# The S5 recurrence on VectorE, its output ahead of fewer gate columns, and mLSTM scores in four tiles

## The chip, the cores and the metric

The kernel runs on one core of a Trainium2 chip. The metric is the device time of one execution in microseconds (us). A core has TensorE (PE), VectorE (DVE), ScalarE (ACT), GpSimd (POOL) and SyncE (SP), each with its own in-order instruction stream; in the profile PEld is the loading of weights into TensorE. DMA transfers are issued from the queues of SP, ACT and POOL.

## The reference

One layer of a hybrid block with D = 2048, 256 latent tokens and 256 context tokens. One projection `w_in` of the modulated inputs feeds three branches: a Hyena long convolution, an mLSTM and an S5 state-space model, each 768 wide. Every branch is projected to 2048 and multiplied by its own sigmoid gate (6144 more columns of `w_in`); the sum goes through `w_out`, and a squared-ReLU MLP follows.

```python
hy_c, qk_c, v_c, o_c, gt_c, u_c, mg_c = jnp.split(h_ctx @ w_in, SPLIT_POINTS, axis=-1)
hy_l, qk_l, v_l, o_l, gt_l, u_l, mg_l = jnp.split(h_lat @ w_in, SPLIT_POINTS, axis=-1)
hm_l, _, _ = mlstm_bidir(mlstm_prep(qk_l, v_l, gt_l, ...), mst_f, mst_b)
ys_l, _, _ = s5_bidir(u_l, disc, c_re, c_im, sst_f, sst_b, True)   # x_t = A x_(t-1) + B u_t, both directions
y = y.reshape(B, L, W_S5) + d * u                                  # s5_out
z = jax.nn.gelu(y); y_s5 = z * jax.nn.sigmoid(z @ glu_w + glu_b)
merged = g_hy * (y_hy @ w_hy_out) + g_ml * (y_ml @ w_ml_out) + g_s5 * (y_s5 @ w_s5_out)
x = layer_norm(ALPHA * x + mod[2] * (merged @ w_out)); x = layer_norm(ALPHA * x + mod[5] * mlp(modulate(x)))
```

## The kernel before

**Weights.** Every large product streams its weight matrix from HBM in chunks of 128x1024 (512 KB) on SP's queue into `wr` (four buffers). ACT rounds a chunk to `wh` (L190) and DVE forms the rest `wl = wr - wh` (L194); each has three buffers. TensorE then does 24 matmuls on a latent chunk (hi x hi, hi x lo, lo x hi; L211). The next chunk's `wh` and `wl` can be written once the matmuls on the buffer's last holder are done.

**Order.** The program runs through the modulation `w_mod`, then the columns of `w_in` for K, V, Q, U and O (U feeds S5), the hyena columns `hy` (36 chunks: blocks hy0 to hy3 of eight chunks and hy4 of four), and the 96 chunks of gate columns, here G0 to G11, eight chunks each, whose results go to DRAM (`mg_consume`, stores L1210 on POOL's queue) until the merges read them back. A merge of a branch multiplies its output by its projection and by its gates. After that come `w_out` and the MLP.

**Sides.** `run_steps(steps, n)` writes n chunks of a matrix into the program; after each chunk every registered side generator is advanced by its rate (`with_side(gen, rate)`), and `drain()` writes out what is left of one. A second side, `mod_late`, runs all along: it accumulates the rest of `w_mod` on DVE (`mac`, L1180, two of 128x512 a chunk of its weights). The program's order isn't the engines' order: a list scheduler (`schedule_with_timeline_sim`) fixes each engine's static order from its own simulation, with the program's order as priority.

**S5.** `u_consume` stores U reordered to DRAM (`UD`) and keeps the latent part in the tile `uT`. `s5_inject` forms the input of the states in `S`; `s5_scan` (L644) is a recurrence of 63 dependent steps, four elementwise instructions of 128x96 each (L651 to L654), on POOL. `s5_output` (L659) works through six column tiles: DMA loads of `u`, `KD` and `Q`, eight small copies of the states into one buffer `xb` (four on ACT, four on DVE, L679), 32 matmuls with `Q` (L686), 16 with `tp` (L692), four ACT copies `ye`, 16 matmuls `aux<-consts` (L211), and one DVE instruction that adds d times `uT` (L701, into `z`). After the sixth tile one Gelu on ACT covers all of `z`. `s5_glu` splits `z` into hi and lo (`s5wq<-z`) and multiplies it by the GLU matrix in six chunks, glu0 and glu1 with three each.

**Placing.** In the program before, `s5_scan` is a side (rate 2) under the last 36 hyena chunks, then 32 gate chunks (G0 to G3) follow, `s5_output` is a side at rate 0.6 under 48 more (G4 to G9), then `s5_glu`, the hyena convolution (`hyena`: short DFT products with elementwise work on DVE and POOL between), the last 16 gate chunks (G10, G11) and the merges. `mlstm` writes its scores into `st_all`, one large tile that shares its buffer with tiles used until the U columns are done.

Of the kernel before, what the change touches and what calls it, by code (L numbers as in the profile page):

```python
# [10 lines left out]
F32 = mybir.dt.float32  # L11
# [6 lines left out]
P = 128  # L18
D = 2048
KT = D // P  # L20
T = 256
W = 768
CT = W // P
DFF = 8192
NIN = 12304
HEADS = 4
DH = 192
LC = 8
# [87 lines left out]
class Kern:  # L116
# [482 lines left out]
    def u_consume(self, ct0, nct, ps):  # L599

        for c in range(nct):
            ct = ct0 + c
            up = self.b2([P, LC, 2, 32])
            self.act(up[:, ::-1], ps[:, 2 * c:2 * c + 2, :].rearrange("p s (j i) -> p i s j", i=LC))
            for g in range(8):
                self.nc.scalar.dma_start(self.UD[ct, :, :, g, :].rearrange("i c n -> c i n"),
                                         up[16 * g:16 * g + 16].rearrange("c i s j -> c i (s j)"))
            self.nc.vector.tensor_copy(self.uT[:, ct, :], ps[:, 2 * c + 1, :])

# [34 lines left out]
    def s5_scan(self):  # L644

        v = self.nc.gpsimd
        S = self.S
# [9 lines left out]
    def s5_output(self):  # L657

        nc = self.nc  # L659
        v = nc.vector  # L660
# [5 lines left out]
        for ct in range(CT):  # L666
            u = self.s5_u(ct, self.b2([P, 8, NCH]))
            tp = self.t(self.br, [P, 8, P], "s5tp", 2)
            nc.scalar.dma_start(tp.rearrange("p g n -> p (g n)"), self.KD[:, :, ct].rearrange("i c g n -> (i c) (g n)"))
            Q = self.t(self.br, [P, 2, 2, 4, P], "s5wq", 2)  # L670
            nc.scalar.dma_start(Q.rearrange("p d s q n -> p d (s q n)"),
                                self.QD[ct].rearrange("d p s q n -> p d (s q n)"))
# [26 lines left out]
            for i in range(LC):  # L699
                self.mm(pc[:, i, :], ye[:, i].rearrange("r p g c -> r (p g c)"), self.c("four"), i == 0, True)  # L700
            v.scalar_tensor_tensor(z[:, ct, :].rearrange("p (j i) -> p i j", i=LC),  # L701
                                   self.uT[:, ct, :].rearrange("p (j i) -> p i j", i=LC),
                                   self.s5d[:, ct:ct + 1], pc, op0=ALU.mult, op1=ALU.add)
# [187 lines left out]
    def mlstm(self):  # L891
        nc = self.nc
        v = nc.vector
        st = []
        st_all = self.t32(F32, (P, 4, HEADS, T))
        for sb in range(4):
            s_sb = st_all[:, sb]
            for hp in range(2):
                ps = self.aux([P, 2, T])
# [506 lines left out]
    def run(self):  # L1406
# [4 lines left out]
        self.MG = self.t(self.dr, [12, P, 4, T], "MG")  # L1411
        self.A8 = self.t(self.dr, [P, 192], "A8")
        self.WA = self.t(self.dr, [CT, P, 4, 4, P], "WA")
        self.QD = self.t(self.dr, [CT, 2, P, 2, 4, P], "QD")
# [48 lines left out]
        with self.scope("yp") as self.yp:  # L1463
# [12 lines left out]
            with self.scope("pA") as self.br:  # L1476
# [26 lines left out]
                self.mlstm()  # L1503
                self.uT = self.ty()
                self.lin_w_all(w_in, O_U, W, KT, both, self.u_consume)
# [9 lines left out]
            with self.scope("pB") as self.br:  # L1515
# [6 lines left out]
                self.run_steps(hy, 36)  # L1522
                self.run_steps(steps, 32)
                self.with_side(self.s5_output(), 0.6)
                self.run_steps(steps, 48)
                self.drain()
# [46 lines left out]
```

## Time and profile before

| | us |
|---|---|
| median of 3 runs (lowest, highest) | 2005.19 (2005.02, 2005.46) |
| the profiled execution | 2014.18 |
| its span | 2012.4 |
| PE busy in the span | 1870.4 (93%) |
| DVE busy | 1300.5 (65%) |
| ACT busy | 803.2 (40%) |
| POOL busy | 361.7 (18%) |

Busy times are of the profiled execution. A row of a timeline gives the start from the beginning of the span, the duration of the group, the engine, the line and what is written from what; PEclk is the granted TensorE clock as a share of full speed. Some stretches of PE's row that count as busy run at half the clock, so busy time and work done are not the same there.

### The profile page before, as it was taken

The numbers are of one execution on the slowest core, as the hardware profiler recorded it, in microseconds if no ns is written. First come the engines' busy times: TensorE is split into PE (matmuls) and PEld (weight loads), VectorE is DVE, ScalarE is ACT, GpSimd is POOL, SyncE is SP. The second block draws the span as 40 slices with busy tenths as digits, with TensorE's granted clock in tenths as the row PEclk, the third lists the DMA queues.
The fourth block names the chain that finished last, engine by engine and source line by source line (L and its number), as shares of the span: only waits on it lengthen the run. The fifth ranks groups of instructions, "written<-read, shape, count | busy, mean of one in ns | idle before, by whom it ended". The sixth has DMA issues, their size and how long they took to land.

```text
span 2012.4 us, 34496 instructions
## 1 busy us (share of the span) xinstructions
PE 1870.4 (93%) x13945; PEld 1707.4 (85%) x13945; DVE 1300.5 (65%) x1810; ACT 803.2 (40%) x1063; POOL 361.7 (18%) x534
## 2 busy tenths in 40 slices
PE   5888999999997995999889998999999999999996
PEld 1666988989997995999779877999988899998985
DVE  8985777647866553556786866766755555555556
ACT  2433324226543333544234533444433344444332
POOL 1221101000019994000452400400000000000001
PEclk7898999999998997999999998999999999999998
DMA  9997667775797765677657866577765566666553
GB/s 346 339 344 262 192 202 220 227 208 174 232 349 230 239 222 210 226 254 259 244 180 253 276 225 227 158 240 224 254 224 187 187 183 186 181 186 231 190 188 105
DMA packets 253472, 455.92 MB, mean 227 GB/s; under 512 B 28597, under 2 KB 75349, under 8 KB 251776
## 3 DMA queue, kind: packets, MB, share of 16 engines
q1 hardware_dynamic: 221824, 382.43, 59.4%
q0 software_dynamic: 14112, 50.83, 7.0%
q10 hardware_dynamic: 17376, 20.45, 3.1%
q8 instruction: 109, 1.79, 0.4%
q14 instruction: 51, 0.42, 0.1%
HBM read 424.75 MB, written 32.05 MB: 227 GB/s over the span
## 4 chain that ended last, share of the span: by engine, by line
PE 67%; DMA 10%; DVE 9%; POOL 8%; issue 3%; ACT 2%; SPq 0%; ACTq 0%; POOLq 0%; DVEq 0%
PE mm L211 59%; PE aux L211 4%; DMA wr<-in_w_mod_dram 4%; DVE wl L194 3%; DMA wr<-in_w_in_dram 2%; POOL sc L651 2%; POOL sc L653 2%; POOL sc L652 2%; POOL t L654 2%; DMA wr<-in_w_out_dram 1%; ACT wh L190 1%; PE px L406 1%; PE px L211 1%; PE aux L214 1%; DVE mac L1180 1%
## 5 line engine op out<-in xcount | busy, mean ns | idle before, releaser
L211 PE MATMUL mm<-t,wh 128*128 128x256 f32 x5888 | 1101.7, 288 | 29.0 <-ACT wh L190 18.1
L211 PEld LDWEIGHTS mm<-t,wh 128*128 128x128 f32 x5888 | 932.2, 194 | 49.6 <-ACT wh L190 19.9
L194 DVE TENSOR_TENSOR wl<-wr,wh 128x1024 fp32r<-128x1024 f32 (+1 forms) x517 | 649.6, 1263 | 385.9 <-ACT wh L190 385.4
L190 ACT ACTIVATE wh<-wr 128x1024 fp32r<-128x1024 f32 (+1 forms) x517 | 545.9, 1058 | 811.0 <-PE mm L211 580.6
L211 PE MATMUL mm<-t,wl 128*128 128x256 f32 x2944 | 847.6, 288 | 13.9 <-DVE wl L194 13.8
L211 PEld LDWEIGHTS mm<-t,wl 128*128 128x128 f32 x2944 | 570.1, 194 | 25.9 <-DVE wl L194 18.3
L1180 DVE SCALAR_TENSOR_TENSOR mac<-wr,vecs,mac 128x512 f32<-128x512 f32 x240 | 185.3, 772 | 156.5 <-DMA wr<-in_w_mod_dram 153.8
L211 PE MATMUL mm<-wh,t 128*128 128x512 f32 (+1 forms) x960 | 249.1, 349 | 0.2
L211 PEld LDWEIGHTS mm<-wh,t 128*128 128x128 f32 x960 | 169.0, 190 | 24.2 <-ACT wh L190 1.6
L211 PE MATMUL mm<-wl,t 128*128 128x512 f32 (+1 forms) x480 | 168.0, 350 | 5.5 <-DVE wl L194 5.5
L211 PE MATMUL mm<-wh,ff 128*128 128x512 f32 (+1 forms) x576 | 155.3, 358 | 0.0
L211 PEld LDWEIGHTS mm<-wh,ff 128*128 128x128 f32 x576 | 101.7, 188 | 17.6
L211 PEld LDWEIGHTS mm<-wl,t 128*128 128x128 f32 x480 | 91.3, 190 | 20.5 <-DVE wl L194 9.2
L211 PE MATMUL mm<-wl,ff 128*128 128x512 f32 (+1 forms) x288 | 103.0, 357 | 0.0
L211 PE MATMUL mm<-ty,wh 128*128 128x256 f32 x384 | 73.3, 289 | 0.0
L1402 POOL DMA_DIRECT2D t<-in_ln_g_dram x1 | 0.5, 535 | 355.0 <-PE mm L211 355.0
L211 PE MATMUL mm<-ty,wl 128*128 128x256 f32 x192 | 56.4, 294 | 7.6 <-DVE wl L194 7.5
L211 PEld LDWEIGHTS mm<-wl,ff 128*128 128x128 f32 x288 | 54.2, 188 | 8.8
L211 PEld LDWEIGHTS mm<-ty,wh 128*128 128x128 f32 x384 | 60.7, 192 | 0.9
L406 PE MATMUL px<-wr,b 128*32 128x512 f32 x128 | 41.4, 739 | 18.1 <-DVE s5t L335 10.5
L211 PE MATMUL aux<-t,t 128*128 128x384 f32 (+3 forms) x160 | 47.3, 411 | 7.7 <-DVE t L1146 3.2
L211 PEld LDWEIGHTS mm<-ty,wl 128*128 128x128 f32 x192 | 36.9, 192 | 9.1 <-DVE wl L194 8.4
(384 smaller groups left out, 1621.6 us busy)
## 6 DMA issues: line engine op xcount, KB each, us to landing
wr<-in_w_ff_dram SPq DMA_DIRECT2D x256, 512.0 KB, 3.9
wr<-in_w_in_dram SPq DMA_DIRECT2D x192, 512.0 KB, 4.7
wr<-in_w_mod_dram SPq DMA_DIRECT2D x160, 512.0 KB, 4.8
wr<-in_w_out_dram SPq DMA_DIRECT2D x32, 512.0 KB, 4.7
wh<-in_w_mod_dram SPq DMA_DIRECT2D x16, 512.0 KB, 7.6
wl<-in_w_mod_dram SPq DMA_DIRECT2D x16, 512.0 KB, 7.1
QD<-s5Q POOLq DMA_DIRECT2D x12, 512.0 KB, 7.1
WA<-s5wa POOLq DMA_DIRECT2D x24, 256.0 KB, 6.2
```

The source lines that it names most:

```text
L190: return self.nc.scalar.activation(out, in_, f, bias=bias, scale=scale)
L194: self.nc.vector.tensor_sub(lo, x, hi.bitcast(F32))
L211: self.nc.tensor.matmul(out, lhsT, rhs, start=start, stop=stop, skip_group_check=True)
L214: self.nc.tensor.transpose(out, in_, self.c("ident", n)[:, :n])
L406: nc.tensor.matmul(ps[o:o + 32], self.st[:, k, :], raw[:, kk, :], start=k < 4, stop=k >= KT - 4, skip_group_check=True, tile_position=(0, o))
L651: v.tensor_mul(t1, self.a8[:, 0], S[:, :, :, :, n - 1])
L652: v.tensor_mul(t2, self.a8[:, 1], S[:, :, ::-1, :, n - 1])
L653: v.tensor_add(t1, t1, S[:, :, :, :, n])
L654: v.tensor_add(S[:, :, :, :, n], t1, t2)
L1180: v.scalar_tensor_tensor(acc, x, c, acc, op0=ALU.mult, op1=ALU.add)
L1402: nc.gpsimd.dma_start(g2r, I["ln2_g"].to_broadcast([P, D]))
```

## The change

Four edits. The recurrence `s5_scan` is issued on DVE instead of POOL. The latent part of U is no longer kept in `uT`: `u_consume` copies it into a short-lived tile and stores it to the DRAM tensor `UL` by POOL's queue (six stores), and `s5_output` loads it back by ACT's queue (six loads). The mLSTM's scores go into four tiles of the pool `ty` in place of the one large tile. And the placing: 16 gate chunks (G0, G1) follow the hyena columns, then `s5_output` is a side at rate 0.4 under 16 more (G2, G3), is drained, and `s5_glu` and the hyena convolution follow; the remaining 64 gate chunks (G4 to G11) come behind them in the program.

```diff
--- before.py
+++ after.py
@@ -605,7 +605,9 @@
             for g in range(8):
                 self.nc.scalar.dma_start(self.UD[ct, :, :, g, :].rearrange("i c n -> c i n"),
                                          up[16 * g:16 * g + 16].rearrange("c i s j -> c i (s j)"))
-            self.nc.vector.tensor_copy(self.uT[:, ct, :], ps[:, 2 * c + 1, :])
+            ul = self.b2([P, T])
+            self.nc.vector.tensor_copy(ul, ps[:, 2 * c + 1, :])
+            self.nc.gpsimd.dma_start(self.UL[ct], ul)
 
     def s5_u(self, ct, u):
 
@@ -643,7 +645,7 @@
 
     def s5_scan(self):
 
-        v = self.nc.gpsimd
+        v = self.nc.vector
         S = self.S
         for n in range(1, NCH):
             t1 = self.t(self.sm, [P, 2, 2, 24], "sc1", 2)
@@ -668,6 +670,8 @@
             tp = self.t(self.br, [P, 8, P], "s5tp", 2)
             nc.scalar.dma_start(tp.rearrange("p g n -> p (g n)"), self.KD[:, :, ct].rearrange("i c g n -> (i c) (g n)"))
             Q = self.t(self.br, [P, 2, 2, 4, P], "s5wq", 2)
+            ul = self.b2([P, T])
+            nc.scalar.dma_start(ul, self.UL[ct])
             nc.scalar.dma_start(Q.rearrange("p d s q n -> p d (s q n)"),
                                 self.QD[ct].rearrange("d p s q n -> p d (s q n)"))
 
@@ -699,7 +703,7 @@
             for i in range(LC):
                 self.mm(pc[:, i, :], ye[:, i].rearrange("r p g c -> r (p g c)"), self.c("four"), i == 0, True)
             v.scalar_tensor_tensor(z[:, ct, :].rearrange("p (j i) -> p i j", i=LC),
-                                   self.uT[:, ct, :].rearrange("p (j i) -> p i j", i=LC),
+                                   ul.rearrange("p (j i) -> p i j", i=LC),
                                    self.s5d[:, ct:ct + 1], pc, op0=ALU.mult, op1=ALU.add)
             yield
         self.dump("s5y", z)
@@ -892,9 +896,8 @@
         nc = self.nc
         v = nc.vector
         st = []
-        st_all = self.t32(F32, (P, 4, HEADS, T))
         for sb in range(4):
-            s_sb = st_all[:, sb]
+            s_sb = self.ty()[:, :HEADS, :]
             for hp in range(2):
                 ps = self.aux([P, 2, T])
                 for hh in range(2):
@@ -1410,6 +1413,7 @@
         self.KD = self.t(self.dr, [LC, 16, CT, 8, P], "KD")
         self.MG = self.t(self.dr, [12, P, 4, T], "MG")
         self.A8 = self.t(self.dr, [P, 192], "A8")
+        self.UL = self.t(self.dr, [CT, P, T], "UL")
         self.WA = self.t(self.dr, [CT, P, 4, 4, P], "WA")
         self.QD = self.t(self.dr, [CT, 2, P, 2, 4, P], "QD")
         self.mrow = self.t(self.dr, [2, D], "mrow")
@@ -1501,7 +1505,6 @@
                 self.drain(2)
                 self.sides[1][1] = 1.5
                 self.mlstm()
-                self.uT = self.ty()
                 self.lin_w_all(w_in, O_U, W, KT, both, self.u_consume)
                 self.sides[1][1] = 0.6
                 self.oT = self.ty()
@@ -1520,9 +1523,9 @@
                 self.sides[1][1] = 0.3
                 self.with_side(self.s5_scan(), 2)
                 self.run_steps(hy, 36)
-                self.run_steps(steps, 32)
-                self.with_side(self.s5_output(), 0.6)
-                self.run_steps(steps, 48)
+                self.run_steps(steps, 16)
+                self.with_side(self.s5_output(), 0.4)
+                self.run_steps(steps, 16)
                 self.drain()
                 self.s5_glu()
             with self.scope("pC") as self.br:
```

The rows below are the engines' static orders; names are those of the program with the buffer's number.

TensorE before, in G4, where the output of S5 starts: the first tile's matmuls (L686, L692) stand in the middle of the gate columns' (`mm<-t,wh` and `mm<-t,wl`), and its `aux<-consts` comes some 30 matmuls later, ahead of the next tile's.

```order
L211 MATMUL mm_8110<-t_20_103,wl_8390 128x256
L211 MATMUL mm_8110<-t_20_103,wh_8472 128x256
L686 MATMUL aux_8200<-s5wq_8190,b_1109_8182 64x128 x16
L692 MATMUL aux_8200<-s5tp_8188,b_1111_8186 32x128 x8
L211 MATMUL mm_8110<-t_20_103,wh_8472 128x256
L211 MATMUL mm_8110<-t_20_103,wl_8473 128x256
```

Some 20 rows further the first tile's `aux<-consts` and the second tile's matmuls stand in the same way:

```order
L211 MATMUL mm_8110<-t_20_103,wl_8560 128x256
L211 MATMUL mm_8110<-t_20_103,wh_8559 128x256
L211 MATMUL aux_8229<-consts_91,b_1110_8184 128x32 x8
L686 MATMUL aux_8313<-s5wq_8303,b_1109_8182 64x128 x16
L692 MATMUL aux_8313<-s5tp_8301,b_1122_8299 32x128 x8
```

Before, every piece of the output has gate columns on both sides.

TensorE after, behind the last matmuls of G3 (`mm_8040`); the rows L690, L696, `aux<-consts` follow six times in all, and then come the GLU's matmuls (`mm<-s5wq,wh`).

```order
L211 MATMUL mm_8040<-t_21_104,wh_8426 128x256 x2
L211 MATMUL mm_8040<-t_21_104,wl_8427 128x256
L211 MATMUL px_8504<-ones_81,mac_7386 128x1 x4
L690 MATMUL aux_7727<-s5wq_7715,b_1061_7707 64x128 x16
L696 MATMUL aux_7727<-s5tp_7713,b_1063_7711 32x128 x8
L211 MATMUL aux_7756<-consts_92,b_1062_7709 128x32 x8
L690 MATMUL aux_7846<-s5wq_7834,b_1061_7707 64x128 x16
L696 MATMUL aux_7846<-s5tp_7832,b_1076_7830 32x128 x8
```

The sixth tile's rows and the GLU's first:

```order
L690 MATMUL aux_8385<-s5wq_8373,b_1061_7707 64x128 x16
L696 MATMUL aux_8385<-s5tp_8371,b_1136_8369 32x128 x8
L211 MATMUL aux_8414<-consts_92,b_1062_7709 128x32 x8
L211 MATMUL mm_8469<-s5wq_8461,wh_8472 128x256
L211 MATMUL mm_8469<-s5wq_8462,wh_8472 128x256
```

The six tiles of S5's output now follow each other on TensorE with no gate column between them, and stand behind G3 and ahead of the GLU and G4.

VectorE before, around hy4 and G0: splits (L194), `mac` (L1180) and the convolution pairs of `hy_consume` (L740, L742).

```order
L194 TENSOR_TENSOR wl_7065<-wr_7062,wh_7064 128x1024
L1180 SCALAR_TENSOR_TENSOR mac_6244<-wr_7170,vecs_93,mac_6244 128x512 x2
L194 TENSOR_TENSOR wl_7107<-wr_7104,wh_7106 128x1024
L194 TENSOR_TENSOR wl_7143<-wr_7140,wh_7142 128x1024
L740 SCALAR_TENSOR_TENSOR b_972_7051<-b_971_7049,vecs_93,b_972_7051 128x4x63
L740 SCALAR_TENSOR_TENSOR b_973_7056<-b_971_7049,vecs_93,b_973_7056 128x4x63
L742 SCALAR_TENSOR_TENSOR b_972_7051<-b_971_7049,vecs_93,b_972_7051 128x4x63
```

VectorE after, between G3's last chunks and the GLU's second: split, `mac` (now L1183) and the recurrence's rows (L653 to L656, the tile `t_686` is `S`), a step of four at a time.

```order
L194 TENSOR_TENSOR wl_8427<-wr_8424,wh_8426 128x1024
L1183 SCALAR_TENSOR_TENSOR mac_7386<-wr_8500,vecs_94,mac_7386 128x512
L656 TENSOR_TENSOR t_686_5307<-sc_968_7006,sc_969_7007 128x96
L653 TENSOR_TENSOR sc_970_7012<-t_686_5307 128x96
L654 TENSOR_TENSOR sc_971_7013<-t_686_5307 128x96
L655 TENSOR_TENSOR sc_970_7012<-sc_970_7012,t_686_5307 128x96
L194 TENSOR_TENSOR wl_8473<-wr_8470,wh_8472 128x1024
L656 TENSOR_TENSOR t_686_5307<-sc_970_7012,sc_971_7013 128x96
L653 TENSOR_TENSOR sc_976_7052<-t_686_5307 128x96
L654 TENSOR_TENSOR sc_977_7053<-t_686_5307 128x96
L655 TENSOR_TENSOR sc_976_7052<-sc_976_7052,t_686_5307 128x96
```

Nearly three of four instructions in this piece belong to the recurrence.

Further down, ahead of the first copies `xb` (L683) that S5's output begins with, the last steps stand behind the split of the GLU's third chunk (`wl_8543`):

```order
L194 TENSOR_TENSOR wl_8543<-wr_8540,wh_8542 128x1024
L656 TENSOR_TENSOR t_686_5307<-sc_987_7107,sc_988_7108 128x96
L1183 SCALAR_TENSOR_TENSOR mac_8621<-wr_8622,vecs_94,mac_8621 128x512
L653 TENSOR_TENSOR sc_989_7113<-t_686_5307 128x96
L654 TENSOR_TENSOR sc_990_7114<-t_686_5307 128x96
L655 TENSOR_TENSOR sc_989_7113<-sc_989_7113,t_686_5307 128x96
L656 TENSOR_TENSOR t_686_5307<-sc_989_7113,sc_990_7114 128x96
L653 TENSOR_TENSOR sc_994_7149<-t_686_5307 128x96
L654 TENSOR_TENSOR sc_995_7150<-t_686_5307 128x96
L683 TENSOR_TENSOR b_1061_7707<-t_686_5307,sign_86 64x4x32 x3
```

The 252 instructions of the recurrence now stand in DVE's stream between hy2 and the output's first copies, one to one and a half steps for each chunk's split.

## Rows read from the trace of the kernel before

**Rows 1.** page, part 1: busy us (share of the span) x instructions.

```profile
PE 1870.4 (93%) x13945; PEld 1707.4 (85%) x13945; DVE 1300.5 (65%) x1810; ACT 803.2 (40%) x1063; POOL 361.7 (18%) x534
```

**Rows 2.** stretches: length, busy us (matmuls) by engine, PEclk, DMA share, GB/s.

```profile
340.00:600.00 260.00, 258.82 (x2271) 244.32 (x2270) 172.93 (x323) 115.22 (x196) 11.00 (x18) 1.00 0.75 234
600.00:620.00 20.00, 15.39 (x112) 14.90 (x111) 12.24 (x17) 8.68 (x14) 15.33 (x27) 0.85 0.74 254
776.00:780.00 4.00, 2.91 (x28) 2.94 (x30) 3.30 (x6) 3.76 (x9) 1.95 (x5) 0.50 0.02 4
800.00:820.00 20.00, 20.00 (x236) 19.14 (x236) 11.82 (x19) 9.02 (x20) 0.54 (x1) 1.00 0.83 289
940.00:1070.00 130.00, 112.53 (x801) 103.05 (x800) 104.69 (x130) 46.63 (x65) 52.65 (x53) 0.95 0.66 226
```

**Rows 3.** timeline of ACT: first copies of a block's sums; hy3, G3, G5.

```profile
611.38 1.02 ACT L190 ACTIVATE b<-mm 128x1024 f32<-128x1024 f32 x1 [2.56 <-PE mm L211]
...
735.62 0.58 ACT L190 ACTIVATE mg<-mm 128x512 f32<-128x512 f32 x1
...
835.12 1.09 ACT L190 ACTIVATE mg<-mm 128x512 f32<-128x512 f32 x2
```

**Rows 4.** waits, 600 to 780: us in total, times, longest.

```profile
PE aux L686 <- POOL sc L651: 21.4, 1, 21.4
```

**Rows 5.** chain of work that ended last: start, us, what.

```profile
777.09 3.68 PE aux L686 x32
780.77 0.87 PE aux L692 x16
...
819.00 1.90 PE aux L686 x32
820.90 0.57 PE aux L692 x16
...
825.26 1.71 PE aux L211 x16
826.97 38.83 PE mm L211 x323
```

**Rows 6.** timeline of DVE, small and large instructions.

```profile
21.38 0.24 DVE L480 TENSOR_TENSOR s5t<-s5pq 128x48 f32<-128x48 f32 x1
21.54 0.23 DVE L481 TENSOR_TENSOR s5t<-s5pq 128x48 f32<-128x48 f32 x1
21.81 0.24 DVE L482 TENSOR_TENSOR s5pq<-s5t 128x48 f32<-128x48 f32 x1
...
596.45 0.74 DVE L1180 SCALAR_TENSOR_TENSOR mac<-wr,vecs,mac 128x512 f32<-128x512 f32 x1
597.12 1.23 DVE L194 TENSOR_TENSOR wl<-wr,wh 128x1024 fp32r<-128x1024 f32 x1
598.27 0.61 DVE L641 TENSOR_TENSOR t<-aux,one 128x64 f32<-128x64 f32 x4
598.79 0.47 DVE L740 SCALAR_TENSOR_TENSOR b<-b,vecs,b 128x252 f32<-128x252 f32 x1
```

**Rows 7.** POOL's groups by form (mean ns); one split beside them on DVE.

```profile
L652 POOL TENSOR_TENSOR sc<-t 128x96 f32<-128x96 f32 x63 | 44.0, 698 | 0.0
...
L654 POOL TENSOR_TENSOR t<-sc,sc 128x96 f32<-128x96 f32 x63 | 31.0, 493 | 4.5
...
623.49 1.47 DVE L194 TENSOR_TENSOR wl<-wr,wh 128x1024 fp32r<-128x1024 f32 x1
```

**Rows 8.** timelines of ACT and DVE, the output's copies and tail.

```profile
813.64 1.57 ACT L190 ACTIVATE b<-aux 32x256 f32<-32x256 f32 x4 [0.59 <-PE aux L692]
...
827.78 1.49 ACT L190 ACTIVATE z<-z 128x1536 f32<-128x1536 f32 x1 [1.80 <-DVE z L701]
...
819.04 0.68 DVE L701 SCALAR_TENSOR_TENSOR z<-ty,vecs,aux 128x256 f32<-128x256 f32 x1
...
831.39 1.82 DVE L194 TENSOR_TENSOR s5wq<-z,s5wq 128x768 fp32r<-128x768 f32 x2
```

## The prediction

> **What bounds the kernel now.** I read the share of busy time first: TensorE is busy for 93% of the span [rows 1], so the question is what its idle and slow stretches are and which of them the change touches. The stretches by engine come next [rows 2]: from 340 to 600 us TensorE stands for 1.2 of 260 us, so nothing that is hidden there can be gained; from 600 to 620 it is busy for 15.4 of 20 us at a clock of 0.85, and from 776 to 780 it runs at 0.50; from 800 to 820 it is full. Hyena and merges (940 to 1070) leave it 17.5 us idle at a clock of 0.95.
>
> What the stretch 611 to 835 is worth is read from three copies on ACT [rows 3]: hy3's sums are copied at 611.38, G3's at 735.62, G5's at 835.12. Between the first and the last lie 223.7 us. The work in it: 4 chunks of hy4 and 48 of gates, the six tiles of S5's output, and two or three groups of some 0.8 us for the modulation (2 us). A chunk's 24 matmuls take 2.885 us, since 323 took 38.83 in the chain [rows 5]: 52 of them are 150.0. One output tile takes 1.90 + 0.57 + 1.71 = 4.18 us of TensorE [rows 5], six 25.1. So 177 us are work and some 47 are stalls and half clock. Of these, 21.4 are one wait: the first matmuls L686 for the recurrence on POOL [rows 4]. The 19 us or so lost before 735.62 (124.2 against 36 chunks, 103.9, and 1 or 2) lie beside POOL's recurrence: there a split on DVE takes 1.47 us [rows 7] where it takes 1.23 alone [rows 6].
>
> **The recurrence on DVE.** It removes 252 instructions from POOL, at 0.49 to 0.70 us each [rows 7], some 160 us, and adds 252 of 96 elements to DVE. No row shows one of 96 elements there. Nearest are 48 elements: starts 0.16 us apart where independent and 0.27 where dependent [rows 6]; 48 elements more cost 0.05 by the larger rows (a split of 1024 elements starts the next 1.15 us later, 596.45 to 597.12 is 0.67 for 512 [rows 6], so some 0.9 ns an element). In a step, two or three of the four wait for the one ahead: from 4 x 0.21 = 0.85 to 4 x 0.32 = 1.3; I take 1.0, since about every fourth instruction has a split between itself and what it needs. 63 us in all.
>
> [...]
>
> Who waits for it: behind these instructions on DVE stand the splits, and TensorE takes a split every 2.885 us. By the order, from hy2's fourth split to the GLU's third there stand 61 steps, 51 splits, 29 `mac` and 10 convolution pairs: 61 x 1.0 + 51 x 1.15 + 29 x 0.67 + 10 x 1.0 [rows 6] = 149 us. TensorE in the same stretch: 48 chunks, 138.5, and 2: 140.5, and some 7 until the GLU's third split. The two engines are even. In-order streams this even, with three buffers between, don't stay hidden wholly: I take 8 us of loss (0 to 20). The old loss of 19 us beside POOL goes.
>
> **The output in one piece.** The order shows that the six tiles stand together on TensorE behind G3, no gate column between. What was hidden before now lies open:
> - Ahead of it: the GLU's third split needs a buffer that G3's last matmuls hold. From there: `wh` 1.05, split 1.15, `mac` 0.67, nine scan instructions some 2.3, four copies `xb` 1.2, and handovers: 7.5 us.
> - First tile, cold, as at 777.09: 3.68 + 0.87 [rows 5], then `ye` 1.57 [rows 8] with 0.4 of handover, 1.71 for `aux<-consts`: 8.4.
> - Five tiles: 1.90 + 0.57, 2.0 for `ye`, 1.71, handover 0.3: 6.5 each, 32.5. The next `xb` fits beside `aux<-consts`.
> - Tail: 0.68 for the last z, Gelu 1.49, the first split of z on ACT and DVE (0.8 and 0.9 by half of 1.82 [rows 8]), handovers: 4.9.
>
> Together 53.3 us; TensorE works in 25.1 of them. The GLU then starts after a pause; at 776 to 780 the clock was 0.50 behind one [rows 2], and a 4 to 6 us stretch of that costs some 3.
>
> New time for the work of 611 to 835: 36 chunks 103.9, modulation 2, DVE loss 8, output 53.3, GLU cold 3, and G4 and G5, now later, 46.2: 216.4 against 223.7, a gain of 7.3.
>
> **Hyena earlier.** Of its 130 us now, 17.5 are idle and the clock is 0.95 [rows 2], a loss of some 20 to 24 us. It moves under plain gate columns G4 to G7. Its own chain (DFT on TensorE, products on DVE and POOL) keeps its waits, and the splits keep their place beside them; only the merges' products no longer stand among it on DVE. I take 2 us of gain (from 7 of gain to 3 of loss).
>
> **U by DRAM and the scores.** The copy on DVE remains, to another tile. Six stores go to POOL's queue, which now has no recurrence in it; six loads go to ACT's queue behind `u` and `KD` and ahead of `Q`, for a tile needed only at the end of each output tile. Nothing, hidden by the matmuls L690. `mlstm` no longer waits for the large tile and moves into the U blocks, where TensorE is full [rows 2]: nothing to gain, and some copies on ACT and DVE land between splits. `wr` loads and the evacuations of hy0 and hy1, which the order puts one split later on ACT, may open gaps of 1 or 2 us. Together 4 us of loss (0 to 8).
>
> Sum: -7.3 - 2 + 4 = -5.3 on the profiled execution of 2014.18 us, which is 0.45% above the median; on the median I take -4, because part of the stalls that go may be what made this execution longer: 2001.
>
> **The rivals.**
> *The clock falls in the output.* Between L690, L696 and `aux<-consts` TensorE pauses some 2.0 and 0.3 us in every tile, six times, and never has two pieces of more than 2.5 us without a pause. [...] For it: the 0.50 at 776 to 780, where TensorE worked for 2.9 of 4 us [rows 2]. Against it: in hyena's 130 us, with 17.5 us of pauses, the clock kept 0.95.
> [...]
>
> *DVE has room.* If a step takes 0.85 us, DVE's 140 us stand at TensorE's 140.5 with the 7 us behind it as slack: the loss of 8 goes, the wait ahead of the output falls from 7.5 to 4, and hyena gains 7 where I took 2: 16.5 us, so 1985. For it: splits stand between most of the dependent instructions. Against it: the fixed order lets three scan instructions in a row wait for each other at many places.
>
> *DVE is the bound.* At 1.3 us a step, DVE needs 168 us where TensorE has 147: 20 us of loss instead of 8, 2013; it shares the slower side with the first.
>
> *The change doesn't do what it says* in one point: the output is not hidden behind gate columns at all, by the order. This is in the forecast, so it has no chance of its own.
>
> **How the numbers follow.** My forecast, 2001 (own range 1994 to 2009): 0.48. Clock or DVE on the slower side, 2011 to 2022: 0.28. DVE with room, 1983 to 1993: 0.24. The range of 1985 to 2021 leaves out the ends of both. A measurement of this kernel tells some 0.2%, 4 us, from no change, so faster is below 2001.2, slower above 2009.2. The forecast stands on that border: 0.22 of its 0.48 faster, 0.20 same, 0.06 slower. With the others: faster 0.46, same 0.20, slower 0.34.
>
> **What would show it.** A scan step near 1.0 us on DVE, all 63 between hy2 and the first L690; TensorE's waits for `wl` in G0 to G3 at some 8 us; no wait of 21 us for the recurrence; L690 to the GLU's first matmul in some 46 us with later L690 groups at 1.9. L690 groups of 3.6 us beyond the first show the clock's rival; splits in G0 to G3 that end long before their matmuls show DVE with room. I am wrong altogether if TensorE's idle time goes to a place that the order doesn't show, such as the transfers of `Q` in the output, which have less time a tile once nothing stands between the tiles.

## The result and the profile after

The changed kernel takes 2031.8 us (median of 4 runs, 2027.45 to 2036.81) against 2005.1 for the kernel before: a ratio of 1.0136, 95% interval 1.0113 to 1.0158, so 27 us slower. The forecast was 2001, its range ended at 2021; the time lies outside.

The profiled executions stand differently to their medians. Before it was the longest shown (2014.18, span 2012.4), after it is the shortest of four (2027.45, span 2025.7). So the two traces differ by 13 us, where the medians differ by 27. The page's first part of after answers to [rows 1]:

```profile
PE 1887.6 (93%) x13945; PEld 1717.8 (85%) x13945; DVE 1349.1 (67%) x2062; ACT 803.6 (40%) x1062; POOL 213.0 (11%) x288
```

POOL has lost its recurrence, DVE gained 49 us, and PE is busy for 17 us longer with the same number of matmuls: part of its busy time ran at a lower clock, 0.67 of full speed on average from 740 to 800 us and 0.50 from 744 to 748.

To place the 13 us I read four copies on ACT in each trace: Q's end, G3's end, the GLU's end and the first copy of the MLP. Before (G3's stands in [rows 3]; the two rows of `mg` are the copies of G8 and G9), then after:

```profile
357.77 0.55 ACT L190 ACTIVATE t<-mm,vecs 128x256 f32<-128x256 f32 x1
...
905.26 1.07 ACT L190 ACTIVATE mg<-mm 128x512 f32<-128x512 f32 x2
928.30 1.06 ACT L190 ACTIVATE mg<-mm 128x512 f32<-128x512 f32 x2
...
943.68 0.82 ACT L190 ACTIVATE b<-mm,vecs 128x256 f32<-128x256 f32 x2
...
1288.43 1.01 ACT L190 ACTIVATE b<-mm 128x1024 f32<-128x1024 f32 x1
```

```profile
358.60 0.55 ACT L190 ACTIVATE t<-mm,vecs 128x256 f32<-128x256 f32 x1
...
738.50 1.06 ACT L190 ACTIVATE mg<-mm 128x512 f32<-128x512 f32 x2
...
817.81 0.85 ACT L190 ACTIVATE b<-mm,vecs 128x256 f32<-128x256 f32 x2
...
1298.85 1.01 ACT L190 ACTIVATE b<-mm 128x1024 f32<-128x1024 f32 x1
```

A block of gate columns takes 23.04 us when nothing disturbs it (905.26 to 928.30 above: eight chunks of 2.88). With the blocks that lie between two marks taken off, the stretches compare:

| stretch, us | before | after |
|---|---|---|
| start to Q's end | 357.8 | 358.6 |
| Q's end to G3 | 377.9 | 379.9 |
| G3 to the GLU's end, less gate blocks (6 before, 0 after) | 69.8 | 79.3 |
| GLU's end to the MLP, less gate blocks (2 before, 8 after) | 298.7 | 296.7 |
| MLP to the end of the span | 724.0 | 726.9 |

The stretches of after by engine (length, busy us of PE, PEld, DVE, ACT and POOL with counts, PEclk, DMA share, GB/s) answer to [rows 2]:

```profile
340.00:600.00 260.00, 251.41 (x2167) 234.89 (x2167) 175.32 (x357) 107.47 (x188) 13.01 (x22) 0.99 0.74 235
600.00:620.00 20.00, 20.00 (x169) 20.00 (x168) 19.67 (x45) 10.69 (x13) 1.38 (x2) 1.00 0.81 251
740.00:760.00 20.00, 11.68 (x112) 10.29 (x112) 9.60 (x30) 5.77 (x19) 0.44 (x1) 0.60 0.60 196
760.00:780.00 20.00, 15.69 (x146) 14.21 (x148) 3.77 (x11) 6.22 (x18) 0.00 (x0) 0.74 0.70 256
780.00:800.00 20.00, 13.39 (x128) 11.87 (x126) 3.05 (x7) 7.86 (x16) 0.54 (x1) 0.67 0.19 63
```

Between 340 and 600 us TensorE now stands for 8.6 us where it stood for 1.2. From 600 to 620 it is full and DVE is at 19.7 of 20. From 740 to 800, the S5 output, its clock is 0.60, 0.74 and 0.67. Output tiles on TensorE (start, length, line), the first two and the third's start:

```profile
745.54 3.66 PE L690 MATMUL aux<-s5wq,b 128*64 128x128 f32 x32 [8.24 <-issue]
749.13 0.64 PE L696 MATMUL aux<-s5tp,b 128*32 128x128 f32 x16
751.61 2.83 PE L211 MATMUL aux<-consts,b 128*128 128x32 f32 x16 [1.84 <-ACT b L190]
754.37 3.68 PE L690 MATMUL aux<-s5wq,b 128*64 128x128 f32 x32
757.98 1.08 PE L696 MATMUL aux<-s5tp,b 128*32 128x128 f32 x16
760.82 1.97 PE L211 MATMUL aux<-consts,b 128*128 128x32 f32 x16 [1.75 <-ACT b L190]
762.72 3.60 PE L690 MATMUL aux<-s5wq,b 128*64 128x128 f32 x32
```

TensorE stands for 8.2 us ahead of the first tile and 1.8 in each tile. L690 takes 3.6 us in every tile, the time that the first, cold group took before [rows 5], and a tile takes 8.35 to 8.8 us. That is the prediction's rival of the clock.

### The profile page after: what moved, and what is told of

It is laid out like the page before. It is cut to its first block, busy times and chain, and to the rows that moved or that the text cites. A ratio compares the mean times of both kernels' runs of the same rounds, so it can differ in the third digit from the quotient of the medians.

```text
span 2025.7 us, 34555 instructions
## 1 busy us (share of the span) xinstructions
PE 1887.6 (93%) x13945; PEld 1717.8 (85%) x13945; DVE 1349.1 (67%) x2062; ACT 803.6 (40%) x1062; POOL 213.0 (11%) x288
## 4 chain that ended last, share of the span: by engine, by line
PE 67%; DMA 14%; DVE 12%; issue 3%; ACT 3%; ACTq 0%; POOL 0%; POOLq 0%; DVEq 0%; SPq 0%
PE mm L211 58%; DMA wr<-in_w_mod_dram 6%; DVE wl L194 5%; PE aux L211 4%; DMA wr<-in_w_in_dram 3%; DMA wr<-in_w_out_dram 2%; ACT wh L190 1%; DMA s5wq<-WA 1%; DVE mac L1183 1%; PE aux L690 1%; PE px L406 1%; PE px L211 1%; PE aux L214 1%; ACT b L190 1%; ACT ty L190 0%
## 5 line engine op out<-in xcount | busy, mean ns | idle before, releaser
L194 DVE TENSOR_TENSOR wl<-wr,wh 128x1024 fp32r<-128x1024 f32 x517 | 646.9, 1256 | 366.8 <-ACT wh L190 365.3
L190 ACT ACTIVATE wh<-wr 128x1024 fp32r<-128x1024 f32 x517 | 545.9, 1058 | 821.0 <-PE mm L211 574.6
L1183 DVE SCALAR_TENSOR_TENSOR mac<-wr,vecs,mac 128x512 f32<-128x512 f32 x240 | 184.7, 770 | 128.7 <-DMA wr<-in_w_mod_dram 126.3
L211 PEld LDWEIGHTS aux<-t,t 128*128 128x128 f32 (+1 forms) x160 | 25.2, 204 | 22.6 <-issue 14.5
```

The lines of the kernel that those rows point to most:

```text
L190: return self.nc.scalar.activation(out, in_, f, bias=bias, scale=scale)
L194: self.nc.vector.tensor_sub(lo, x, hi.bitcast(F32))
L211: self.nc.tensor.matmul(out, lhsT, rhs, start=start, stop=stop, skip_group_check=True)
L1183: v.scalar_tensor_tensor(acc, x, c, acc, op0=ALU.mult, op1=ALU.add)
```

## Experiments: the four edits apart

**e1, the scores alone**, on the kernel before.

```diff
-        st_all = self.t32(F32, (P, 4, HEADS, T))
-            s_sb = st_all[:, sb]
+            s_sb = self.ty()[:, :HEADS, :]
```

> Only the mLSTM scores are changed (four tiles of the pool ty instead of one large one); the recurrence stays on GpSimd and the placing is that of before. Theory A (the changed kernel loses in two places: the mLSTM that now runs inside the U columns, where TensorE was full, and the S5 output in one piece): TensorE stands 7 us or more longer between 340 and 600 us than before, and the kernel takes 2012 to 2020 us. Rival B (the loss is in the S5 output alone, the mLSTM's new place is free): 2003 to 2007 us, TensorE idle in 340 to 600 at some 1 us.

Measured: 2011.1 us against 2008.6, ratio 1.0015 (1.0003 to 1.0027). Theory A's 2012 to 2020 was wrong in the time. A part of its mechanism is there: between 340 and 600 us TensorE stands for 6.6 us where before it stood for 1.2, somewhat less than the 7 us more that the theory asked for. But POOL's recurrence begins at 571 us instead of 602 and is waited for less. The states' copies on ACT wait for it, a split stands behind them, and TensorE waits for that split for 15.9 us, where the first tile of before waited 21.4 [rows 4]:

```profile
751.25 0.80 PE L211 MATMUL mm<-t,wh 128*128 128x256 f32 x2 [15.94 <-ACT wh L190]
```

The loss of 5.4 and the gain of 5.5 cancel.

**e2, the recurrence alone on DVE**, on the kernel before.

```diff
     def s5_scan(self):
-        v = self.nc.gpsimd
+        v = self.nc.vector
```

> Only the recurrence is moved to VectorE; the scores, the tile uT and the placing are those of before. By the order the six pieces of the S5 output then lie between the gate columns of G5 and G6, some 30 matmuls apart. Theory A: the losses of before beside GpSimd's recurrence (some 19 us) and the wait for it (21 us and the slow clock after it) go, and some 8 to 12 us of waits for the splits come: 1965 to 1985 us. Rival C (VectorE, not the placing, is what made the changed kernel slow): no gain, 2000 us or more, with TensorE waiting for wl in hy3 to G4 for 20 us or more.

Measured: 1984.1 us, ratio 0.9887 (0.9865 to 0.9909): 23 us faster. Moving the recurrence is good; rival C falls. It is at the upper end of theory A, on which more below.

**e3, the changed kernel with the placing of before.**

```diff
-                self.run_steps(steps, 16)
-                self.with_side(self.s5_output(), 0.4)
-                self.run_steps(steps, 16)
+                self.run_steps(steps, 32)
+                self.with_side(self.s5_output(), 0.6)
+                self.run_steps(steps, 48)
```

> The changed kernel with the placing of before (32 gate chunks, the output at rate 0.6 under 48 more, hyena ahead of the last 16); recurrence on VectorE, U through DRAM and scores in four tiles stay. Theory A: the output is hidden between gate columns again, the some 39 us that TensorE idles or runs slowly around it fall to under 5: 1985 to 2000 us. Rival C (VectorE is the bound): 2020 us or more.

Measured: 1995.9 us, ratio 0.9932 (0.9911 to 0.9953). With nothing but the placing undone, 1.0136 becomes 0.9932: the placing costs 2.0%, some 41 us. By the two traces, which are not at their medians, it is 30 us (spans of 2025.7 and 1995.3), and 28 of them lie between G3 and the GLU's end (79.3 against 51.1 in the table below).

**e4, the changed kernel with the old scores.**

```diff
+        st_all = self.t32(F32, (P, 4, HEADS, T))
-            s_sb = self.ty()[:, :HEADS, :]
+            s_sb = st_all[:, sb]
```

> The changed kernel with the mLSTM scores in one large tile again, all else as changed. Theory A: TensorE's idle time between 340 and 600 us falls from 8.6 us to 1 or 2 and the kernel takes 2014 to 2024 us instead of 2032. Rival B (the mLSTM's place is free): 2027 to 2037 us as the changed kernel.

Measured: 2035.1 us, ratio 1.0137 (1.0106 to 1.0168): no difference, as rival B said, but not for its reason. In e4's trace the recurrence begins at 600 us instead of 576, and the output's first tile waits 16.6 us instead of 8.2:

```profile
747.73 3.68 PE L690 MATMUL aux<-s5wq,b 128*64 128x128 f32 x32 [16.56 <-issue]
751.34 1.08 PE L696 MATMUL aux<-s5tp,b 128*32 128x128 f32 x16
754.26 3.59 PE L211 MATMUL aux<-consts,b 128*128 128x32 f32 x16 [1.84 <-ACT b L190]
757.78 3.68 PE L690 MATMUL aux<-s5wq,b 128*64 128x128 f32 x32
```

What the scores cost ahead of it they win back as an earlier recurrence. This trace also shows how the output varies: here `aux<-consts` ran at 3.6 us too, and a tile took 10.0 us where the trace of after shows 8.35 to 8.8.

**e5, recurrence on DVE and U through DRAM**: e3 with the old scores (or e2 with `UL`).

```diff
+        st_all = self.t32(F32, (P, 4, HEADS, T))
-            s_sb = self.ty()[:, :HEADS, :]
+            s_sb = st_all[:, sb]
```

> Recurrence on VectorE and U through DRAM, with the scores and the placing of before: between the run with the recurrence alone (1984 us) and the one with the scores too (1996 us) it has one edit more than the first and one less than the second. If the mLSTM's new place costs those 12 us (theory A): 1981 to 1988 us, TensorE idle between 340 and 600 us for 1 or 2 us. If U through DRAM costs them: 1993 to 1999 us.

Measured: 1980.0 us, ratio 0.9873 (0.9848 to 0.9898), as e2 within the intervals. U through DRAM costs nothing that these runs can tell. The scores cost 0.6%, some 12 us, when they come on top of e5 (e3).

Taken in this order (e2, e5, e3, the changed kernel), the steps are: recurrence on DVE -23 us, `UL` nothing (-3, inside the intervals), scores +12, placing +41; together +27. In other company an edit has another price: the scores cost 3 us in e1 and nothing in e4.

## Experiments: why the placing costs

**e6, the output's pauses filled**: the changed kernel with eight idle matmuls a tile (two instructions each in the trace), where TensorE waits for `ye`; of the first tile's sixteen, fourteen went ahead of it.

```diff
             pc = self.aux([P, LC, 32])
+            for _ in range(8):
+                self.mm(pc[:, 0:4, :].rearrange("p i j -> p (i j)"), self.c("ident"), self.c("ident"), True, True)
```

> The changed kernel with eight more matmuls (identity times identity, 128 columns) in each of the six output tiles, written ahead of the sixteen aux<-consts and into the same sums, which overwrite them: TensorE works on nothing useful while it would wait for the copies ye. If the pauses are why the clock is low in the output (the clock's rival of the prediction): the later L690 groups take 1.9 us instead of 3.6, a tile 6.3 to 7 us instead of 8.6 to 10, and the kernel 2010 to 2022 us instead of 2032. If the low clock has another cause (the shape of these matmuls): L690 stays at 3.6 and the kernel becomes slower, by 8 to 15 us, since the added matmuls take longer than the pause.

Measured: 2023.8 us, ratio 1.0076 (1.0051 to 1.0101): 8 us at the median less than the changed kernel (12 by the ratios, whose intervals lie apart), with more work. The time lies 2 us above the range that was expected; L690 and the tiles came out about as expected. The third tile of e6 and the fourth's L690, and the stretch 756 to 786 by engine:

```profile
762.52 1.97 PE L690 MATMUL aux<-s5wq,b 128*64 128x128 f32 x32
764.42 0.64 PE L696 MATMUL aux<-s5tp,b 128*32 128x128 f32 x16
765.00 2.05 PE L211 MATMUL aux<-consts 128*128 128x128 f32 x16
766.88 1.91 PE L211 MATMUL aux<-consts,b 128*128 128x32 f32 x16
768.72 1.97 PE L690 MATMUL aux<-s5wq,b 128*64 128x128 f32 x32
```

```profile
756.00:786.00 30.00, 30.00 (x374) 27.61 (x372) 7.32 (x20) 12.37 (x36) 0.54 (x1) 0.95 0.67 232
```

L690 is at 1.97 us, a tile at 6.2, and the clock at 0.95. From G3 to the GLU's end there are 71.9 us instead of 79.3 (e4: 95.9). The pauses are the only thing that was changed, and with them filled the clock is 0.95, where after has 0.67 from 740 to 800 us. Whether a pause as such keeps it low, or that a tile alone holds too little work, this run can't tell apart, since it put full matmuls into the pause. Of the 28 us that the placing costs in this stretch by the traces, some 7 are the clock; the other 21 are the chain that lies open.

**e7, 32 gate chunks, the output under 24**: e2 with

```diff
-                self.run_steps(steps, 48)
+                self.run_steps(steps, 24)
```

> The kernel before with the recurrence on VectorE and another placing: 32 gate chunks, the output at rate 0.6 under 24 more (so that by the order its six tiles lie some 30 gate matmuls apart), then the GLU and the hyena convolution, then the last 40; scores and uT as before. Theory A: as the recurrence alone (1984 us) or better by what hyena gains under plain gate columns, 2 to 5 us: 1978 to 1986 us. If hyena under gate columns keeps its loss: 1984 to 1990 us.

Measured: 1980.5 us, ratio 0.9868 (0.984 to 0.9896), as e2 within the intervals.

**e8, the changed placing 16 chunks later**, with the old scores.

```diff
-                self.run_steps(steps, 16)
+                self.run_steps(steps, 32)
                 self.with_side(self.s5_output(), 0.4)
                 self.run_steps(steps, 16)
```

> Recurrence on VectorE, U through DRAM, scores as before, and the changed placing shifted by 16 chunks: 32 gate chunks, the output at rate 0.4 under 16 more, then GLU, hyena and the last 48. By the order five of the six output tiles lie between gate columns; the last one, the Gelu and the split lie open ahead of the GLU. Theory A (what lies open is what costs): 8 to 12 us for the last tile and the tail, less 2 to 5 for hyena, against the run with the recurrence alone: 1988 to 1996 us.

Measured: 1987.9 us, ratio 0.991 (0.9886 to 0.9934). Five of six tiles lie between gate chunks and only the last, the Gelu and the split lie open. The median lies just below the range expected and 0.4% behind e5, but the intervals overlap.

In e5 every tile has gate columns on both sides. Its chain of waits (start, us, what) shows L690 at 1.90 us and 3.79 us of gate matmuls where after has a pause, and from G3's end to the GLU's TensorE is busy for 180.75 of 183 us at a clock of 1.00:

```profile
781.47 1.90 PE aux L690 x32
783.37 0.57 PE aux L696 x16
783.94 3.79 PE mm L211 x30
787.72 1.71 PE aux L211 x16
789.43 1.90 PE aux L690 x32
```

```profile
728.00:911.00 183.00, 180.75 (x1665) 177.32 (x1666) 112.26 (x174) 86.03 (x128) 7.86 (x15) 1.00 0.80 263
```

Marks of e5 on ACT, for the table below:

```profile
353.24 0.55 ACT L190 ACTIVATE t<-mm,vecs 128x256 f32<-128x256 f32 x1
...
726.92 1.07 ACT L190 ACTIVATE mg<-mm 128x512 f32<-128x512 f32 x2
...
910.63 0.82 ACT L190 ACTIVATE b<-mm,vecs 128x256 f32<-128x256 f32 x2
```

| us | before | after | e3 | e4 | e5 | e6 |
|---|---|---|---|---|---|---|
| Q's end to G3 | 377.9 | 379.9 | 380.8 | 375.0 | 373.7 | 383.3 |
| G3 to the GLU's end, less gate blocks | 69.8 | 79.3 | 51.1 | 95.9 | 45.5 | 71.9 |

**e11, e7 with U through DRAM**, whose core is

```diff
-            self.nc.vector.tensor_copy(self.uT[:, ct, :], ps[:, 2 * c + 1, :])
+            ul = self.b2([P, T])
+            self.nc.vector.tensor_copy(ul, ps[:, 2 * c + 1, :])
+            self.nc.gpsimd.dma_start(self.UL[ct], ul)
```

> Recurrence on VectorE, U through DRAM, scores as before; 32 gate chunks, the output at rate 0.6 under 24 more, GLU, hyena, the last 40. U through DRAM costs nothing and hyena's earlier place is worth 2 us at most (theory A): 1976 to 1982 us. If U through DRAM and the placing each gained on their own: 1972 to 1976 us.

Measured: 1978.6 us, ratio 0.9851 (0.9835 to 0.9867). It, e5 and e7 aren't told apart by their intervals; all three beat both kernels.

## Experiments: what was lost ahead of G3

The first row of the table asks a question. The prediction put 19 us lost before G3 down to the recurrence on POOL. With the recurrence on DVE (e5) the stretch from Q's end to G3 gained 4 us.

**e9, no recurrence at all**: e5 with its side left out (the states stay what the inputs made them).

```diff
-                self.with_side(self.s5_scan(), 2)
```

> The run with the recurrence on VectorE and U through DRAM (1980 us), with the 63 steps left out: the states stay what the inputs made them, so S5's output isn't the reference's. It measures what the recurrence still costs on VectorE. By the prediction's term (8 us of waits for the splits): 1970 to 1975 us. If VectorE is nearer to the bound than the prediction took it (15 us or more, as the stretch from Q to G3 suggests, which gained 4 us where 11 were forecast): 1960 to 1967 us.

Measured: 1974.2 us, ratio 0.9835 (0.9811 to 0.9858), 6 us less than e5 with intervals that just overlap; the stretch takes 366.3. So the recurrence on DVE costs 6 or 7 us, close to the 8 of the prediction, and something else stays.

**e12, fewer mac beside the recurrence**: e11 with

```diff
-                self.sides[1][1] = 0.3
+                self.sides[1][1] = 0.1
                 self.with_side(self.s5_scan(), 2)
 ...
+                self.sides[1][1] = 0.4
                 self.with_side(self.s5_output(), 0.6)
```

> As e11, with the modulation's side at rate 0.1 instead of 0.3 while the recurrence runs (hyena columns and G0 to G3) and at 0.4 from the output on: about two thirds of the mac instructions, some 15 to 20 of 0.67 us, leave the stretch in which VectorE is full. If VectorE bounds that stretch: TensorE's waits for wl there shrink and the kernel takes 1966 to 1975 us. If not: 1976 to 1982 us.

Measured: 1986.9 us, ratio 0.9891 (0.9873 to 0.9909), slower than e11 and than both ranges expected; but the stretch falls to 356.1 us, and there (520 to 713) TensorE is full:

```profile
520.00:713.00 193.00, 192.95 (x1884) 191.54 (x1883) 164.59 (x391) 94.56 (x136) 16.54 (x27) 1.00 0.82 263
```

What it wins is lost in hyena and the merges: from the GLU's end to the MLP e12 takes 429 us with 12 more `mac`, e11 411 (marks read as above). What waits in the trace of before, which answers to [rows 4] (us in total, times, longest):

```profile
DVE mac L1180 <- DMA wr<-in_w_mod_dram: 27.9, 9, 4.2
...
ACT wh L190 <- DMA HX<-b: 11.8, 1, 11.8
```

The nine waits of `mac` for the modulation's weights hold DVE for 27.9 us, and the splits queue behind. The prediction had counted the `mac` by their 0.67 us and not by this wait. The second row is POOL's part: by the profile a split on ACT waits 11.8 us for a store `HX`, which is queued on POOL among the recurrence's instructions.

The wait on DVE isn't the only way in which the modulation can cost time. Its chunks come by the same queue and into the same four buffers `wr` as those of `w_in`. In e5 (607 to 727 us), where `mac` waits less, ACT waits for the chunks of `w_in` themselves:

```profile
ACT wh L190 <- DMA wr<-in_w_in_dram: 21.3, 9, 4.0
...
DVE mac L1184 <- DMA wr<-in_w_mod_dram: 7.9, 8, 2.0
```

In e11 that first wait is 41.4 us, in e12 it is gone. Moving the `mac` takes their time, their waits and their loads out of the stretch together; which of the three costs most no run here separates.

**e15, the same in the kernel before**, with POOL's recurrence.

```diff
-                self.sides[1][1] = 0.3
+                self.sides[1][1] = 0.1
                 self.with_side(self.s5_scan(), 2)
                 self.run_steps(hy, 36)
                 self.run_steps(steps, 32)
+                self.sides[1][1] = 0.4
                 self.with_side(self.s5_output(), 0.6)
```

> The kernel before (recurrence on GpSimd) with the modulation's side at 0.1 instead of 0.3 while the recurrence runs and 0.4 from the output on. The prediction put the 19 us that TensorE lost between 611 and 736 us down to GpSimd's recurrence. If they are the mac instructions' wait for DMA (28 us in that stretch of before, theory D): that stretch loses under 8 us more than the matmuls need; the wait for the recurrence on GpSimd grows by what was won, so the whole takes 2000 to 2012 us. If GpSimd's own load on VectorE is the cause: the stretch keeps 15 us or more of loss.

Measured: 2011.2 us against 2008.1, ratio 1.0012 (0.9997 to 1.0028); `mac` on this line now waits 5.3 us between 608 and 723 (2.3 more on another line), and the wait for the recurrence is 23.8 us instead of 21.4:

```profile
DVE mac L1180 <- DMA wr<-in_w_mod_dram: 5.3, 3, 2.9
```

```profile
PE aux L686 <- POOL sc L651: 23.8, 1, 23.8
```

The stretch takes 366.0 us, and from hy3's copy to G3's (608.20 to 722.98, 114.8 us) 11 us are lost where before lost 20: neither theory's number. With e9 and e12 this makes a table, in us from Q's end to G3:

| | on POOL | on DVE | none |
|---|---|---|---|
| `mac` at rate 0.3 | 377.9 | 373.7 | 366.3 |
| `mac` at rate 0.1 | 366.0 | 356.1 | not run |

Both causes are there: some 12 to 18 us go with the `mac` (20 if e12 is set against e11, from which it was made), 4 to 10 with the move from POOL to DVE. Each number is from one trace, and kernels with the same rate and the recurrence on DVE differ by 4 us in this stretch (e2 372.2, e11 376.5), so the smallest of these is no more than that. In e15 10 of the 12 us won ahead of G3 are still there at the GLU's end (932.59 - 356.95 against 943.68 - 357.77) and are lost behind it, 7 up to the MLP, with some 6 more `mac`, and 3.5 in it, with 4 more.

**e13 and e14, the mac moved to U and O**: e11 with the rates below; e14 has 2.5, 1.2, 0.1 and 0.2.

```diff
-                self.sides[1][1] = 1.5
+                self.sides[1][1] = 2.0
 ...
-                self.sides[1][1] = 0.6
+                self.sides[1][1] = 1.0
 ...
-                self.sides[1][1] = 0.3
+                self.sides[1][1] = 0.1
                 self.with_side(self.s5_scan(), 2)
 ...
+                self.sides[1][1] = 0.3
                 self.with_side(self.s5_output(), 0.6)
```

> As e11 (1979 us), with the modulation's side moved: rate 2.0 instead of 1.5 in the U columns and 1.0 instead of 0.6 in O, where TensorE had no idle time, 0.1 while the recurrence runs, 0.3 from the output on. If the mac instructions that wait for their weights' DMA are what delays the splits beside the recurrence (theory D): the stretch from Q's end to G3 falls by some 15 us as in e12, and hyena keeps e11's time: 1962 to 1970 us. If the transfers' total rate bounds the stretch from V to hyena as a whole: 1974 to 1982 us.

> As e13, with rates 2.5 in U, 1.2 in O, 0.1 beside the recurrence and 0.2 afterwards, so that hyena has fewer mac beside it than in e11. Theory D: a few us less than e13, 1958 to 1968 us, unless U and O get gaps of their own. Total rate: 1974 to 1985 us.

Measured: 1979.8 us, ratio 0.9855 (0.9839 to 0.9872), and 1998.4 us, ratio 0.9946 (0.9927 to 0.9965). Nothing is won by the first, and the second, above both ranges expected, loses 20 us against e11. In e13 the U and O columns take 5 and 3 us longer than in e11 (85.3 for 80.0, 57.3 for 53.9), and from Q's end to G3 it wins 4 us in place of 15; e14 takes 382.3 us there. Theory D's forecast fails: the `mac` and their loads cost wherever these runs put them (e12: 18 us more than e11 from the GLU's end to the MLP; e13: 5 and 3 in U and O). Why stays open; no run here measured what the transfers share.

**e10, the mLSTM behind U**: e3 with

```diff
-                self.mlstm()
                 self.lin_w_all(w_in, O_U, W, KT, both, self.u_consume)
+                self.mlstm()
```

> The changed kernel with the placing of before (1996 us) and the call of the mLSTM behind the U columns in the program; the scores stay in four tiles. By the order the mLSTM's matmuls then lie in the O and hyena columns, as before the change. If its place inside the U columns is what costs 12 to 16 us: 1978 to 1986 us. If the four tiles cost it (buffers of the pool ty): 1993 to 1999 us.

Measured: 2001.5 us, ratio 0.9981 (0.9965 to 0.9996), above both ranges expected and 0.5% slower than e3; Q's end to G3 takes 381.1 us. So the mLSTM's place in the U columns isn't what the four tiles cost. What is stays open; that the four tiles fill the whole pool `ty`, which has four buffers, was not tried apart.

This run also says what sets the recurrence's start. It begins at 597 us here, as with the old scores (597 in e5, 600 in e4), though there is no large tile; in e3 it begins at 573. So the start goes with the mLSTM's place, and the large tile held back S5 only by holding back the mLSTM.

## Why the prediction was wrong

**Where the miss lies.** By the traces 5 us of gain were forecast and 13 of loss came. From Q's end to G3 a gain of 6 was forecast (some 10 by the old loss less DVE's, less 4 for the scores), and 2 us of loss came. From G3 to the GLU's end 3 of loss were forecast (the cold GLU), and 9.5 came. Hyena came as forecast. The start and the MLP are 4 us longer together, for which the change gives no reason. So two steps failed, by some 8 and 7 us; what the medians add is told under the base, below.

**The clock in the output, one failed step.** The prediction saw from the order that the output lies open, in one piece, and priced it at 53.3 us plus 3 for the cold GLU; with the GLU itself (15.4 us, 928.30 to 943.68 before) that is 71.7 from G3 to the GLU's end. With the clock up (e6) it is 71.9: the wait some 8 for 7.5, a later tile 6.2 for 6.5, the first 10.1 (with the added matmuls in it) for 8.4, and the tail shorter. So the sum was right, in part by errors that offset each other, and the step that failed is that the clock comes back after the first tile. The rival, "the clock falls in the output", is a part of the forecast's 2011 to 2022. At the times of the cold first tile [rows 5] five tiles would lose some 19 us, an estimate: 3.68 - 1.90, 0.87 - 0.57 and, if `aux<-consts` doubles as L690 does, 1.7 in each. No run shows these 19; the trace of after has 7.4 of it, e4's some 16 (95.9 less 71.9 and the 8.3 us of longer wait). Even with the clock up e6 is 15 us slower than before (1.0076), so the clock alone didn't turn the forecast. The evidence against it was hyena, with 17.5 us of pauses at a clock of 0.95. That row was another case: there the pauses lie among gate matmuls, here a tile has nothing else. The row for it, 0.50 at 776 to 780 [rows 2], was the nearer one, though it lies behind a wait of 21 us. In the output the waits are 1.75 to 1.84 us in tiles of 8.35 to 8.8, and L690 still starts cold, at 3.6 us, in all six tiles.

**What the old loss was, the other failed step.** "The old loss of 19 us beside POOL goes" failed. Moving the recurrence won 4 us of Q's end to G3 in e5 where 11 were forecast: the `mac` and their loads were a part of the loss (12 to 18 us by e15 and e12), their wait stood in the waits of before, and it wasn't read. It cost the forecast 7 us.

**DVE.** A step was put at 1.0 us. Where nothing stands between, it takes 1.18 (739.35 to 740.53 in e4's trace: start, length):

```profile
739.35 0.32 DVE L656 TENSOR_TENSOR t<-sc,sc 128x96 f32<-128x96 f32 x1
739.71 0.32 DVE L653 TENSOR_TENSOR sc<-t 128x96 f32<-128x96 f32 x1
739.95 0.32 DVE L654 TENSOR_TENSOR sc<-t 128x96 f32<-128x96 f32 x1
740.18 0.32 DVE L655 TENSOR_TENSOR sc<-sc,t 128x96 f32<-128x96 f32 x1
740.53 0.32 DVE L656 TENSOR_TENSOR t<-sc,sc 128x96 f32<-128x96 f32 x1
```

Starts are 0.24 us apart for independent and 0.36 for dependent instructions, where 0.21 and 0.32 were worked out. The mean here is 0.295 (1.18 by four): the forecast was 15% low for a lone step, and it mattered little. TensorE's wait for `wl` in the stretch 600 to 740 of after is 5.4 us:

```profile
PE mm L211 <- DVE wl L194: 5.4, 5, 1.7
```

8 were forecast, and leaving the recurrence out gives 6 (e9). This term was right, and the rivals that hung on DVE fell both ways.

**U through DRAM, hyena.** Nothing and -2 us were forecast; nothing (e5 against e2) and -2.0 (298.7 to 296.7) were measured. The second agreement is luck: e5 and e2, which leave hyena where it was, have 296.3 and 295.6 us in the same stretch (e5: 910.63 to 1253.01, less two gate blocks).

**The scores.** 4 us of loss with the rest were forecast, 12 measured where the placing hides the output (e3 against e5), nothing where it doesn't (e4), because the recurrence then begins 24 us earlier and is waited for 8 us less. The prediction had not seen that edge: the mLSTM, late as long as it waited for the large tile, held back S5's input (e10).

**The base.** The forecast took less of the gain for the median, since the profiled execution of before was long. The difference of the medians was larger than that of the traces, by 13 us. Part of that is the clock, which differs from execution to execution: over the whole span it is 0.962 in the two faster runs of after (2027, 2029) and 0.959 in the two slower ones (2034, 2037), and a tile takes 8.35 to 8.8 us in the trace of after, up to 10.0 in e4's. The rest isn't accounted for.

## What to carry to other kernels

Work that is written in one piece on TensorE can cost more than its own time: here its chain of waits lay open (21 us by the traces), and the clock was 0.60 to 0.74 for the whole piece (some 7 us). Leave some 30 matmuls of a large product between the steps of such a chain, as e5 has them at a clock of 1.00, and put the chain where its input is surely ready; here that alone was worth 41 us by the medians. And read what an engine waits for as well as what it does: accumulations of 0.67 us waited 3 us each for their loads here, and taking 23 of 85 of them, with their loads, out of a stretch made it 12 to 18 us shorter, though the time was lost again where they went.

## What was not expected of the hardware

With TensorE standing for 1.8 us in each tile of 8.35 to 8.8, the granted clock stayed at 0.60 to 0.74 over 60 us and L690 at 3.6 us in each tile; sixteen idle instructions in the pause brought 0.95 and 1.97. On DVE the starts of 96-element instructions lie 0.24 and 0.36 us apart against 0.16 and 0.27 for 48 elements [rows 6], 1.7 to 1.9 ns an element, about twice what the rows of 512 and 1024 elements gave. The two differ in more than length: the 96 elements are read and written in strides through `S`, and no run here separates that.
